# Moving 215 stores of a hybrid encoder layer from the sync queue to GpSimd's queue

## The chip, the cores and the metric

The kernel runs on one core of a Trainium2 chip. The metric is the device time of one execution in microseconds. A core has engines that run side by side, each through its own instruction list in order: TensorE (PE in the profile, PEld for its weight loads), VectorE (DVE), ScalarE (ACT), GpSimd (POOL) and SyncE (SP), which does nothing but issue transfers. A transfer between the chip's memory and the core's on-chip memory (a DMA) is started by an instruction in the list of SP, ACT or POOL; the issue takes a fraction of a microsecond there, and the bytes are moved by 16 DMA engines that all lists share. An instruction waits on semaphores until what it needs is there, and everything behind it in the same list waits with it.

## The reference

One layer of an encoder over 2048 positions of width 1024, in float32:

```python
u = _rms_norm(h, norm_mix_g[l])
proj = u @ w_in[l]
hy = _short_conv_centred(proj[..., :HY_COLS], hy_conv_w[l], hy_conv_b[l])
spec = _hyena_filter_spectrum(L, ...)          # filters from a small sine network, their rfft
y_hy = _group_rms_norm(_hyena(hy, spec, hy_skip[l]), hy_norm_g[l], HYENA_GROUPS)
qk = jax.nn.silu(_short_conv_centred(proj[..., HY_COLS:off], ml_conv_w[l], ml_conv_b[l]))
y_ml = _mlstm_bidirectional(q, k, v, o_pre, gates, ml_gate_b[l])
mixed = jnp.concatenate([y_hy, y_ml normed by group], axis=-1)
h = h + mixed @ w_out[l]
h = h + _cross_attention(_rms_norm(h, norm_x_g[l]), _rms_norm(mem, norm_mem_g[l]), ...)
h = h + jnp.square(jax.nn.relu(_rms_norm(h, norm_ff_g[l]) @ ff_w1[l])) @ ff_w2[l]
return _rms_norm(h, final_norm_g)
```

`_hyena` multiplies spectra twice (order 0 and 1): z is transformed, multiplied by the filter's spectrum, transformed back and gated. `_mlstm_bidirectional` is a linear recurrence over chunks with a matrix state per head, run forwards and backwards and summed.

## The kernel before

The large products run in float32 split into a rounded high part and a low part, three passes of TensorE each (`mm3`: L355, L358, L359); ScalarE makes the high parts and VectorE the low ones (L366).

Ahead of attention, two streams are woven together. The first is the input projection in halves of 1024 positions: `sweep` takes 256 columns at a time, keeps them channel-major, adds the width-3 convolution (L796 to L803), and `sweep_out` turns the result with TensorE (L825, L831, L845, L855) into staging tiles `st`, which go to memory: `hy` (convolved channels, L828 and L834), `qt` and `kt` (queries and keys, L837) and `kn` (keys the other way round, L849 and L858). `natural` projects values, output gates (`vd`, `od`, L896) and scan gates (`gt`, L903). The second stream is the filters (`filters`: their spectra leave as `fs` through `by_phase`, L339) and then `hyena`. In `hyena`, `spectrum` transforms eight blocks of z on TensorE, copies the result (L998) and stores it as `zs` (L339, through `by_phase`). When all blocks are there, a pass over 16 frequency blocks loads `zs` and `fs` (L920), transforms (L1030), multiplies by the filter (L1034 on VectorE, L1035 on GpSimd, their sum L1036 on VectorE), transforms back (L987), copies (L988) and stores `zg` (L989). Then `zg` is loaded again (L339 as a load), with the gate rows from `hy` (L974). This happens twice; the second time ends with the normed result `yh` (L1060 and L1066 on GpSimd, store L1068).

The gate scans (`gates`) give coefficient rows (`rows`, L1161 and L1162). `backward` makes the states of the backward recurrence from the last chunk to the first: GpSimd scales values (L1196), TensorE multiplies (L1200), VectorE adds (L1206), and the state goes out as `cbd` (L1219). `memproj` projects the memory for attention, with its weights loaded in `raw_stream` (L415). `mlstm` makes the outputs of 16 chunks; GpSimd multiplies rows (L1290), adds masks (L1291) and applies the output gate (L1343); after every second chunk the results are normed (VectorE, L1356) and stored as `ym` (L1358). Attention loads `yh` and `ym` (L1473); most of `mlstm` is woven with attention.

The program is written with a tile framework: a tile name has a fixed number of buffers, an instruction that writes into a used buffer waits until its readers (stores too) are done, and the framework adds those waits. A scheduler in that framework sets the order of each engine's list from a timeline of its own, so the order in the lists is not that of the code. Loads are issued by the sync queue. Before the change GpSimd issues the stores of `zg`, `vd`, `od`, of half the `zs`, and of the memory's projections (`gd`, `vw`); the sync queue issues the other stores of these stages.

Of the kernel before, what the change touches and what calls it, by code (L numbers as in the profile page):

```python
# [128 lines left out]
class Prog:  # L129
# [102 lines left out]
    def filters(self):  # L232
        nc, tc, a = self.nc, self.tc, self.a
        sd = [self.dram(f"fs{o}", (16, 64, 4, CH)) for o in range(2)]
        sb, ta, tb = self.fsb, self.ta, self.tb
        if True:
# [68 lines left out]
            def front(es, st, o, j2):  # L305
                pp = [self.hy() for q in range(4)]
                self.beside(*((pp[q][64 * jj + 32 * p:64 * jj + 32 * p + 32], f1[32 * q:32 * q + 32, 32 * p:32 * p + 32],
                               es[jj][p][32 * q:32 * q + 32]) for q in range(4) for jj in range(2) for p in range(2)))
                for h in range(2):
                    for i in range(2):  # L310
                        nc.scalar.copy(st[h][:, i], pp[2 * h + i])
                    self.by_phase(nc.sync, sd[o], j2, h, st[h])

            nxt = windows(0)
            for j2 in range(8):
# [499 lines left out]
    def sweep_out(self, ct, cv, t0, n):  # L815
# [3 lines left out]
        if ct < 12:  # L819
            w = min(n // 8, 128)  # L820
            dst = self.d_hy[ct // 4, t0:t0 + 8 * w, cc].rearrange("(q j) c -> q j c", j=8)
            for j4 in range(2):
                pt = self.mm().rearrange("p (k t) -> p k t", k=4)
                for jj in range(4):
                    nc.tensor.transpose(pt[0:w, jj], cv[:, 4 * j4 + jj:8 * w:8], self.ident)  # L825
                st = self.ist.tile([128, 4, 128], F32, tag="st", name="st", bufs=3)
                self.copy(st[0:w], pt[0:w])
                nc.sync.dma_start(out=dst[:, 4 * j4:4 * j4 + 4], in_=st[0:w])  # L828
            if n > 8 * w:
                pt = self.mm()  # L830
                nc.tensor.transpose(pt[0:16, 0:128], v[:, 8 * w:n], self.ident)  # L831
                st = self.ist.tile([128, 4, 128], F32, tag="st", name="st", bufs=3)
                self.copy(st[0:16, 0], pt[0:16, 0:128])
                nc.sync.dma_start(out=self.d_hy[ct // 4, t0 + 8 * w:t0 + n, cc], in_=st[0:16, 0])  # L834
            return
        h = ct % 4
        nc.sync.dma_start(out=(self.d_qt if ct < 16 else self.d_kt)[h, :, t0:t0 + n], in_=v)  # L837
        if ct < 16:
            return
        for b in range(0, n, 512):  # L840
            pt = self.mm().rearrange("p (k t) -> p k t", k=4)
            st = self.ist.tile([128, 4, 128], F32, tag="st", name="st", bufs=3)
            full = min(4, (n - b) // 128)
            for jj in range(full):
                nc.tensor.transpose(pt[:, jj], v[:, b + 128 * jj:b + 128 * jj + 128], self.ident)  # L845
            if full:
                self.copy(st[:, 0:full], pt[:, 0:full])
                r0 = t0 + b
                nc.sync.dma_start(out=self.d_kn[r0:r0 + 128 * full, cc].rearrange("(j q) c -> q j c", q=128),  # L849
                                  in_=st[:, 0:full])  # L850
            rest = min(512, n - b) - 128 * full
            if rest:
                s0 = b + 128 * full
                pt = self.mm()
                nc.tensor.transpose(pt[0:rest, 0:128], v[:, s0:s0 + rest], self.ident)  # L855
                st = self.ist.tile([128, 4, 128], F32, tag="st", name="st", bufs=3)
                self.copy(st[0:rest, 0], pt[0:rest, 0:128])
                nc.sync.dma_start(out=self.d_kn[t0 + s0:t0 + s0 + rest, cc], in_=st[0:rest, 0])  # L858

    def natural(self, hf, tiles, after=None, at=4):  # L860
        nc, a, sb = self.nc, self.a, self.isb
# [2 lines left out]
        for c2 in tiles:  # L864
# [3 lines left out]
            for t in range(8):  # L868
# [28 lines left out]
                if c2 == 3:  # L897
# [2 lines left out]
                    nc.vector.tensor_tensor(sg[:, t], p[:, 256:272], self.gb, ALU.add)  # L900
                    if t == 7:
                        dst = self.d_gt[1024 * hf:1024 * hf + 1024]
                        nc.sync.dma_start(out=dst.rearrange("(t p) g -> p t g", p=128), in_=sg)  # L903

    def hyena(self, es):
        nc, tc, a = self.nc, self.tc, self.a
# [84 lines left out]
        def spectrum(o, j2, z):  # L991
# [5 lines left out]
                for h in range(2):  # L997
                    (nc.vector.tensor_copy if h else nc.scalar.copy)(st[h][:, i], pp[2 * h + i])  # L998
            for h in range(2):
                self.by_phase(nc.sync if h else nc.gpsimd, sds[o], j2, h, st[h])  # L1000

        q, fq = [load1(0), load1(1)], []
        yield 52
# [9 lines left out]
        for o in range(2):  # L1013
# [27 lines left out]
            for j2 in range(8):  # L1041
# [34 lines left out]
    def gates(self):  # L1076
# [4 lines left out]
        with tc.tile_pool(name="m_g", bufs=1) as sg:  # L1081
# [79 lines left out]
            nc.sync.dma_start(out=rows[0], in_=negM)  # L1161
# [47 lines left out]
    def backward(self, sb, first, last, old, pin=None, lean=False):  # L1209
# [3 lines left out]
        for n in range(first, last, -1):  # L1213
# [13 lines left out]
    def mlstm(self, es):  # L1227
# [71 lines left out]
        for n in range(16):  # L1299
# [51 lines left out]
            if n % 2:  # L1351
                rv = self.bank_rsqrt(sb, ss, 128)
                for i, y in enumerate(ys):
                    t0 = 128 * (n - 1 + i)
                    for h in range(4):
                        nc.vector.scalar_tensor_tensor(y[:, h], y[:, h], rv[:, 4 * i + h:4 * i + h + 1],  # L1356
                                                       gml[:, 128 * h:128 * h + 128], ALU.mult, ALU.mult)
                    stores.append(lambda t0=t0, y=y: nc.sync.dma_start(  # L1358
                        out=ym[t0:t0 + 128].rearrange("t (h e) -> t h e", h=4), in_=y))
            if n < 14:  # L1360
                ld.append(loads(n + 2))
# [831 lines left out]
```

## Time and profile before

| | us |
|---|---|
| median of 3 runs | 3070.66 |
| lowest and highest run | 3070.19, 3076.88 |
| the profiled execution | 3074.8 |
| its span, from first to last instruction | 3073.1 |

| engine | busy us | share of the span |
|---|---|---|
| TensorE | 2981.7 | 97% |
| TensorE weight loads | 2367.8 | 77% |
| VectorE | 1947.8 | 63% |
| ScalarE | 1491.4 | 49% |
| GpSimd | 1213.7 | 39% |

In the profile a line such as `L339` is a line of the kernel; `a<-zg` says that tile a is written from tensor zg; `SPq` and `POOLq` are the lists of SP and POOL while they only wait or issue. Issuing does not count as busy. The granted clock is TensorE's, as a share of full speed. Attention begins at about 1170 us, and until about 1525 us the last chunks of `mlstm` are woven into it.

### The profile page before, as it was taken

To read this page: it belongs to the slowest core of one execution; us is meant where nothing else is said; L and a number is where in the kernel's file an instruction comes from. 1 tells how busy PE (TensorE), PEld (TensorE's weight loads), DVE (VectorE), ACT (ScalarE), POOL (GpSimd) and SP (SyncE) were. 2 spreads that over 40 slices of the span, in tenths; PEclk is the share of its full clock that TensorE was granted. 3 is DMA by queue.
4 is the path that set the end of the run, shared out by engine and by line. 5 is a ranking of instruction groups with operands and counts; after the bars stand their busy time and mean duration, and the time that the engine had idled before them with its cause. 6 is when DMAs were issued, how large, how long until landed. Compare 5 with 4: busy or idle time off the path is not lost.

```text
span 3073.1 us, 44126 instructions
## 1 busy us (share of the span) xinstructions
PE 2981.7 (97%) x14799; PEld 2367.8 (77%) x14799; DVE 1947.8 (63%) x3442; ACT 1491.4 (49%) x2930; POOL 1213.7 (39%) x942
## 2 busy tenths in 40 slices
PE   9999999998999898999999999999999999999998
PEld 7666667775678667888887888888888888888876
DVE  8855555556755547868665666558555676566695
ACT  6443455634754235555544455556555443333335
POOL 0112113310333544333133247765565374344653
PEclk9999999999999998999999999999999999999999
DMA  6655677586877986564567466657544565344434
GB/s 225 194 188 173 209 250 232 185 275 198 268 218 220 328 286 206 159 223 134 186 205 256 152 209 217 206 182 249 189 154 153 186 199 172 116 159 120 155 103 164
DMA packets 427867, 607.03 MB, mean 198 GB/s; under 512 B 38894, under 2 KB 232302, under 8 KB 426616
## 3 DMA queue, kind: packets, MB, share of 16 engines
q1 hardware_dynamic: 406644, 546.43, 55.6%
q0 software_dynamic: 12544, 41.95, 3.8%
q10 hardware_dynamic: 8452, 15.83, 1.4%
q8 instruction: 117, 1.92, 0.3%
q14 instruction: 110, 0.90, 0.1%
HBM read 401.67 MB, written 202.41 MB: 197 GB/s over the span
## 4 chain that ended last, share of the span: by engine, by line
PE 82%; DMA 7%; DVE 5%; issue 2%; ACT 2%; POOL 1%; SPq 1%; DVEq 0%; ACTq 0%; POOLq 0%
PE mm L355 17%; PE mm L358 17%; PE mm L359 17%; PE hy L359 6%; PE hy L355 6%; PE hy L358 6%; PE hy L173 2%; PE hy L1030 2%; PE mm L956 2%; PE hy L987 1%; DMA va<-vd 1%; DMA a<-zg 1%; PE hy L1322 1%; PE hy L1324 1%; PE mm L825 1%
## 5 line engine op out<-in xcount | busy, mean ns | idle before, releaser
L1692 ACT CAST ah<-w 128x512 fp32r<-128x512 f32 x284 | 176.5, 622 | 300.5 <-PE hy L358 155.9
L1693 DVE TENSOR_TENSOR bl<-wr,bh 128x512 fp32r<-128x512 f32 x213 | 240.0, 1131 | 125.4 <-ACT bh L1692 125.0
L366 DVE TENSOR_TENSOR wl<-wn,wh 128x512 fp32r<-128x512 f32 (+1 forms) x296 | 215.6, 772 | 90.9 <-ACT wh L366 90.6
L355 PE MATMUL mm<-xh,wh 128*128 128x512 f32 x640 | 266.6, 418 | 1.9 <-ACT xh L366 1.0
L358 PE MATMUL mm<-xl,wh 128*128 128x512 f32 x640 | 255.1, 399 | 4.6 <-DVE xl L366 4.6
L359 PE MATMUL mm<-xh,wl 128*128 128x512 f32 x640 | 254.4, 398 | 0.0
L1692 ACT CAST bh<-wr 128x512 fp32r<-128x512 f32 x232 | 143.6, 621 | 228.3 <-PE mm L359 174.3
L1693 DVE TENSOR_TENSOR al<-w,ah 128x512 fp32r<-128x512 f32 x236 | 217.4, 922 | 57.0 <-ACT ah L1692 57.0
L355 PE MATMUL mm<-bh,ah 128*128 128x512 f32 x576 | 225.8, 392 | 1.4 <-DVE acc L1854 1.3
L359 PE MATMUL mm<-bh,al 128*128 128x512 f32 x576 | 223.8, 391 | 3.4 <-DVE al L1693 3.4
L358 PE MATMUL mm<-bl,ah 128*128 128x512 f32 x576 | 224.9, 390 | 0.0
L366 ACT CAST wh<-wn 128x512 fp32r<-128x512 f32 (+1 forms) x296 | 164.6, 620 | 103.9 <-PE mm L359 50.1
L358 PE MATMUL mm<-act,wh 128*128 128x512 f32 x512 | 201.9, 394 | 0.0
L355 PE MATMUL mm<-act,wh 128*128 128x512 f32 x512 | 198.6, 394 | 1.4 <-ACT wh L366 1.3
L359 PE MATMUL mm<-act,wl 128*128 128x512 f32 x512 | 199.5, 392 | 0.1
L355 PE MATMUL hy<-bh,ah 128*128 128x512 f32 x448 | 175.2, 391 | 0.0
L358 PE MATMUL hy<-bl,ah 128*128 128x512 f32 x448 | 174.6, 390 | 0.0
L359 PE MATMUL hy<-bh,al 128*128 128x512 f32 x448 | 174.4, 390 | 0.0
L331 POOL TENSOR_TENSOR b<-b 128x512 f32<-128x512 f32 x32 | 48.1, 1504 | 293.3 <-DVE b L330 273.7
L355 PEld LDWEIGHTS mm<-xh,wh 128*128 128x128 f32 x640 | 121.6, 190 | 52.0 <-issue 21.2
L358 PEld LDWEIGHTS mm<-xl,wh 128*128 128x128 f32 x640 | 121.7, 190 | 51.3 <-issue 20.2
L355 PE MATMUL mm<-wh,xh 128*128 128x256 f32 (+1 forms) x512 | 155.1, 303 | 1.2 <-DVE a L960 1.2
(390 smaller groups left out, 8210.0 us busy)
## 6 DMA issues: line engine op xcount, KB each, us to landing
wr<-hc SPq DMA_DIRECT2D x224, 256.0 KB
w<-in_ff_w_dram SPq DMA_DIRECT2D x172, 256.0 KB
hc<-wn SPq DMA_DIRECT2D x128, 256.0 KB
wn<-in_w_in_dram SPq DMA_DIRECT2D x100, 256.0 KB
hc<-q SPq DMA_DIRECT2D x96, 256.0 KB
fs<-a SPq DMA_DIRECT2D x32, 512.0 KB
a<-fs SPq DMA_DIRECT2D x64, 256.0 KB
a<-zs SPq DMA_DIRECT2D x64, 256.0 KB
```

The source lines that it names most:

```text
L173: b = self.nc.tensor.matmul(*products[-1], start=True, stop=True)
L331: nc.gpsimd.tensor_tensor(b, f, b, ALU.subtract)
L355: first = mm(ps, lh, rh, start=start, stop=False)
L358: mm(ps, lh, rl, start=False, stop=False)
L359: self.last = mm(ps, ll, rh, start=False, stop=stop)
L366: both = (self.nc.scalar.copy(hi, src), self.nc.vector.tensor_tensor(lo, src, hi.bitcast(F32), ALU.subtract))
L825: nc.tensor.transpose(pt[0:w, jj], cv[:, 4 * j4 + jj:8 * w:8], self.ident)
L956: nc.tensor.matmul(pp, dm[:, m], t[:, m], start=True, stop=True)
L987: nc.tensor.matmul(pg, em[:, m], y, start=True, stop=True)
L1030: nc.tensor.matmul(pp, dm[:, m], t[:, m], start=True, stop=True)
L1692: self.nc.scalar.copy(hi, src)
L1693: eng.tensor_tensor(lo, src, hi.bitcast(F32), ALU.subtract)
```

## The change

Every store of the stages ahead of attention that the sync queue issued is now issued by GpSimd: `fs`, `hy`, `qt`, `kt`, `kn`, `gt`, the other half of `zs`, `yh`, `rows`, `cbd` and `ym`. The sync queue keeps the loads there, and the stores of attention and after it.

```diff
 filters
-                    self.by_phase(nc.sync, sd[o], j2, h, st[h])
+                    self.by_phase(nc.gpsimd, sd[o], j2, h, st[h])
 sweep_out
-                nc.sync.dma_start(out=dst[:, 4 * j4:4 * j4 + 4], in_=st[0:w])
+                nc.gpsimd.dma_start(out=dst[:, 4 * j4:4 * j4 + 4], in_=st[0:w])
-        nc.sync.dma_start(out=(self.d_qt if ct < 16 else self.d_kt)[h, :, t0:t0 + n], in_=v)
+        nc.gpsimd.dma_start(out=(self.d_qt if ct < 16 else self.d_kt)[h, :, t0:t0 + n], in_=v)
-                nc.sync.dma_start(out=self.d_kn[r0:r0 + 128 * full, cc].rearrange("(j q) c -> q j c", q=128),
+                nc.gpsimd.dma_start(out=self.d_kn[r0:r0 + 128 * full, cc].rearrange("(j q) c -> q j c", q=128),
...
 hyena, spectrum
-                self.by_phase(nc.sync if h else nc.gpsimd, sds[o], j2, h, st[h])
+                self.by_phase(nc.gpsimd, sds[o], j2, h, st[h])
 hyena, results
-                    nc.sync.dma_start(out=yh[q, :, js], in_=sq[phase[q]])
+                    nc.gpsimd.dma_start(out=yh[q, :, js], in_=sq[phase[q]])
 gates
-            nc.sync.dma_start(out=rows[0], in_=negM)
-            nc.sync.dma_start(out=rows[1], in_=inter)
+            nc.gpsimd.dma_start(out=rows[0], in_=negM)
+            nc.gpsimd.dma_start(out=rows[1], in_=inter)
 backward
-            self.nc.sync.dma_start(out=cbd[n - 1], in_=new.rearrange("d h e -> d (h e)"))
+            self.nc.gpsimd.dma_start(out=cbd[n - 1], in_=new.rearrange("d h e -> d (h e)"))
 mlstm
-                    stores.append(lambda t0=t0, y=y: nc.sync.dma_start(
+                    stores.append(lambda t0=t0, y=y: nc.gpsimd.dma_start(
```

The scheduler makes the lists anew. GpSimd's list gets 215 instructions more and the sync queue's 215 fewer; TensorE's, VectorE's and ScalarE's instructions are the same in number and differ in order in places up to about 1320 us. Three places follow.

GpSimd's list where the first pointwise pass of `hyena` begins. Before:

```order
L339 DMA zs_2736<-a 128x1024 x8
L1035 TENSOR_TENSOR b<-b,a 128x512 x3
L989 DMA zg_2738<-a 16x8x512 x2
L1035 TENSOR_TENSOR b<-b,a 128x512
L989 DMA zg_2738<-a 16x8x512
L1035 TENSOR_TENSOR b<-b,a 128x512
L989 DMA zg_2738<-a 16x8x512
```

and after:

```order
L837 DMA kt<-cv 128x1008
L849 DMA kn<-st 128x4x128
L849 DMA kn<-st 128x3x128
L1035 TENSOR_TENSOR b<-b,a 128x512 x2
L858 DMA kn<-st 112x128
L849 DMA kn<-st 128x4x128
L849 DMA kn<-st 128x3x128
L858 DMA kn<-st 112x128
L1035 TENSOR_TENSOR b<-b,a 128x512
L989 DMA zg_2738<-a 16x8x512 x2
L1035 TENSOR_TENSOR b<-b,a 128x512
```

The stores of keys, which wait for copies of the turned tiles, now stand between the products.

The sync queue's list where the second transform's blocks are handed over (zs_2737 is the second order's transform, fs_391 its filter). Before:

```order
L339 DMA zs_2737<-a 128x1024
L828 DMA hy<-st 128x4x128
L1161 DMA rows<-negM 128x128
L828 DMA hy<-st 128x4x128
L1162 DMA rows<-inter 128x128
L834 DMA hy<-st 16x128
L920 DMA a<-zs_2737 128x1x512 x2
L920 DMA a<-fs_391 128x1x512 x2
```

and after:

```order
L920 DMA a<-zs_2737 128x1x512 x2
L944 DMA dm<-in_c_dm_dram 128x256
L920 DMA a<-fs_391 128x1x512 x2
L920 DMA a<-zs_2737 128x1x512 x2
L949 DMA em<-in_c_em_dram 128x256
```

The stores that stood ahead of the first zs loads are gone from this list.

GpSimd's list in `mlstm`, around the end of the second chunk. Before:

```order
L1343 TENSOR_TENSOR ht<-ht,og 128x512
L739 DMA vw<-o 128x2x256 x3
L1291 TENSOR_TENSOR rw<-rw,mask_9881 128x512
L1290 TENSOR_TENSOR rw<-rw,qn 128x512
L1291 TENSOR_TENSOR rw<-rw,mask_9886 128x512
L1290 TENSOR_TENSOR rw<-rw,qn 128x512
L1343 TENSOR_TENSOR ht<-ht,og 128x512
```

and after:

```order
L1343 TENSOR_TENSOR ht<-ht,og 128x512
L1358 DMA ym<-ht 128x512 x2
L1291 TENSOR_TENSOR rw<-rw,mask_9881 128x512
L1290 TENSOR_TENSOR rw<-rw,qn 128x512
L1291 TENSOR_TENSOR rw<-rw,mask_9886 128x512
L1290 TENSOR_TENSOR rw<-rw,qn 128x512
L1343 TENSOR_TENSOR ht<-ht,og 128x512
```

The two stores of results, which wait for VectorE's norming (L1356), now stand ahead of the next chunk's mask additions; the last stores of the memory's values have moved to an earlier place.

More of the change, by code (lines that the diff above doesn't have):

```diff
@@ L833, in sweep_out @@
                 self.copy(st[0:16, 0], pt[0:16, 0:128])
-                nc.sync.dma_start(out=self.d_hy[ct // 4, t0 + 8 * w:t0 + n, cc], in_=st[0:16, 0])
+                nc.gpsimd.dma_start(out=self.d_hy[ct // 4, t0 + 8 * w:t0 + n, cc], in_=st[0:16, 0])
             return
         h = ct % 4
-        nc.sync.dma_start(out=(self.d_qt if ct < 16 else self.d_kt)[h, :, t0:t0 + n], in_=v)
+        nc.gpsimd.dma_start(out=(self.d_qt if ct < 16 else self.d_kt)[h, :, t0:t0 + n], in_=v)
         if ct < 16:
@@ L857, in sweep_out @@
                 self.copy(st[0:rest, 0], pt[0:rest, 0:128])
-                nc.sync.dma_start(out=self.d_kn[t0 + s0:t0 + s0 + rest, cc], in_=st[0:rest, 0])
+                nc.gpsimd.dma_start(out=self.d_kn[t0 + s0:t0 + s0 + rest, cc], in_=st[0:rest, 0])
     def natural(self, hf, tiles, after=None, at=4):
@@ L902, in natural @@
                         dst = self.d_gt[1024 * hf:1024 * hf + 1024]
-                        nc.sync.dma_start(out=dst.rearrange("(t p) g -> p t g", p=128), in_=sg)
+                        nc.gpsimd.dma_start(out=dst.rearrange("(t p) g -> p t g", p=128), in_=sg)
     def hyena(self, es):
```

## The prediction

> **What bounds the kernel now.** I read the page first, then the windows by stage, then who waits for whom, on TensorE and on the sync queue.
>
> ```profile
> span 3073.1 us, 44126 instructions
> PE 2981.7 (97%) x14799; PEld 2367.8 (77%) x14799; DVE 1947.8 (63%) x3442; ACT 1491.4 (49%) x2930; POOL 1213.7 (39%) x942
> PE 82%; DMA 7%; DVE 5%; issue 2%; ACT 2%; POOL 1%; SPq 1%; DVEq 0%; ACTq 0%; POOLq 0%
> ```
>
> TensorE is the bound: 97% of the span, and 82% of the chain that ended last. What a change of queues can win or lose is TensorE's idle time in the stages whose stores move. The windows (columns: the stretch in us; its length; the busy times of TensorE, its weight loads, VectorE, ScalarE and GpSimd, with their instructions; granted clock; DMA share; GB/s) show where that is:
>
> ```profile
> 0.00:100.00 100.00, 97.46 (x432) 78.53 (x433) 83.90 (x208) 68.85 (x128) 0.68 (x6) 0.98 0.69 227
> 100.00:350.00 250.00, 243.68 (x1504) 164.35 (x1502) 154.27 (x239) 104.74 (x175) 48.14 (x32) 0.99 0.51 169
> 350.00:700.00 350.00, 336.84 (x1948) 248.87 (x1949) 192.63 (x305) 183.98 (x322) 83.68 (x96) 0.99 0.77 246
> 700.00:750.00 50.00, 37.33 (x205) 22.92 (x204) 39.39 (x145) 23.61 (x41) 2.14 (x4) 0.91 0.67 211
> 750.00:1000.00 250.00, 246.63 (x1261) 183.45 (x1260) 152.13 (x259) 142.09 (x240) 87.50 (x90) 0.99 0.74 226
> 1000.00:1150.00 150.00, 138.03 (x695) 103.40 (x694) 66.98 (x206) 47.24 (x132) 78.80 (x78) 0.98 0.93 306
> 1150.00:1200.00 50.00, 36.32 (x215) 32.66 (x216) 35.98 (x124) 26.50 (x100) 18.91 (x16) 0.83 0.68 226
> ```
>
> Length less the first number, summed over the seven rows, is 2.5 + 6.3 + 13.2 + 12.7 + 3.4 + 12.0 + 13.7 = 63.8 us: the ceiling of any gain. The fourth row is the gate stage, where a serial chain on VectorE rules (39.4 of 50 us). In the sixth the DMA engines are 93% busy. The sync queue does wait in front of its stores, with loads behind them (columns: total us, times, longest):
>
> ```profile
> SPq L339 <- ACT a L311: 77.2, 25, 11.5
> SPq L828 <- ACT st L201: 55.2, 21, 5.8
> SPq L1358 <- DVE ht L1356: 24.9, 14, 6.1
> SPq L837 <- ACT cv L801: 23.0, 3, 11.2
> ...
> PE hy L1030 <- DMA a<-zs: 8.8, 3, 4.4
> ...
> PE hy L987 <- DVE b L1036: 2.1, 1, 2.1
> ```
>
> The four sync rows make 180 us of waiting, but the costliest wait of TensorE for a load is 8.8 us, and that one is for a store to land and its data to be read back. The loads behind the held stores are mostly early enough. So I expect little from freeing the sync queue, and look for what the GpSimd queue costs.
>
> **The change part by part.** By the code it moves 215 stores: 32 of the filters, 60 of the convolution (48 full, 12 of 16 rows), 16 of queries and keys, 24 of transposed keys, 2 of gates, 16 of the forward transforms, 32 and 16 of the two results, 2 of rows, 15 of states. No bytes change.
>
> ```profile
> L828 SPq DMA_DIRECT2D hy<-st x48: 309/371/1860, 73.3 to 743.3; - x48
> L989 POOL DMA_DIRECT2D zg<-a x64: 530/553/631, 437.2 to 953.7; - x64
> L896 POOL DMA_DIRECT2D od<-st x16: 717/740/764, 473.1 to 1006.7; - x16
> ```
>
> Issuing (ns, least/median/most): 371 on sync, whatever the pieces; on GpSimd 553 for 128 pieces of a row and 740 for 256, so 0.19 us per further 128 pieces. A store of 512 pieces (hy, kn) is not in the trace as a GpSimd store; below it is no cheaper than the 740 ns row, above four times 553 = 2.2 us; I take 0.74 + 2 x 0.19 = 1.1 us, on the line of the two rows. All 215 then take some 150 us of GpSimd's time, against 880 us in which it is not busy before 1200 us (the seven rows show it busy 320 us). The issue time as such is covered; what counts is what stands behind it.
>
> *First hand-over of the transforms, 411 to 420 us.* The last zs stores must land before the first zs load:
>
> ```profile
> 413.99 0.34 SPq L339 DMA_DIRECT2D zs<-a  x1
> ...
> 416.83 1.17 SPq L920 DMA_DIRECT2D a<-zs  x2
> ...
> DMA to landing us min/median/max: 3.4/3.5/3.5
> ```
>
> From the sync queue the last store was landed after at most 416.83 - 413.99 = 2.84 us; the two GpSimd zs stores of these same microseconds took 3.4 to 3.5 (third row, zs on line 339 between 400 and 425 us). TensorE waits at this point, so the change costs **+0.6**; at most +1.5 with the longer issue ahead of it.
>
> *Second hand-over, 740 us.* Here the sync queue itself is late:
>
> ```profile
> 740.28 0.33 SPq L339 DMA_DIRECT2D zs<-a  x1
> ...
> 742.00 1.18 SPq L1161 DMA_DIRECT2D rows<-negM  x1
> ...
> 745.24 1.17 SPq L920 DMA_DIRECT2D a<-zs  x2
> ...
> 740.41 0.54 POOL L339 DMA_DIRECT2D zs<-a  x1 [6.05 <-ACT a L998]
> ```
>
> The last landing is that of the GpSimd store. It took 3.9 us:
>
> ```profile
> DMA to landing us min/median/max: 3.9/3.9/3.9
> ```
>
> So the data was there at 744.3, and the load went out at 745.24, behind five hy and rows stores. After the change both zs stores go out one behind the other on GpSimd (740.3 and 740.8), the second lands at 744.7, and no store holds the load: **-0.5** (between -0.9 and 0).
>
> *Products behind stores.* In the two pointwise passes GpSimd multiplies (L1035) for VectorE's sum (L1036), which feeds TensorE's L987. Between the products the changed order puts 14 full kn stores (1.1 us each), 8 partial (0.5), 7 of queries and keys and 6 of states (0.55 each, as 128 pieces) and one of the gates (1,024 pieces, 1.9): 15.4 + 4 + 3.9 + 3.3 + 1.9 = 28 us, in what was 64 products and their zg, od and vd stores.
>
> ```profile
> L1035 POOL TENSOR_TENSOR b<-b,a x64: 1262/1293/3907, 423.6 to 944.9; 128x512 f32<-128x512 f32 x64
> ...
>   ACT b L1033: 90.7, 43
> ...
>   DVE b L1036: 14.2, 32
> ```
>
> GpSimd was idle 90.7 us ahead of 43 of its 64 products, 2.1 us each, waiting for ScalarE: about half of the stores fall into that. The other 14 us come late to VectorE, which waited for half of the products already (32 of 64, 14.2 us in all). Of those 14.2 us TensorE felt 2.1 (row L987 above), 15%. At the same share 14 us cost **+2**; the bounds are 0 (all hidden) and +14 (VectorE passes on all of it).
>
> By the Trainium skill (SBUF — State Buffer, "SBUF: two separate sides") a VectorE operation in a two-port mode locks GpSimd out of the port with which it writes descriptors, so that its DMAs wait. The trace has 64 zg stores in stages where VectorE is busy 55 to 60%, and none took over 631 ns to issue, so it does not bear the rule out; if the rule held, the result would be that of rival D.
>
> *Results of the recurrence.* Two ym stores now stand in GpSimd's queue behind L1343 of each second chunk, ahead of the masks (L1291) of the next, and wait for VectorE's eight L1356:
>
> ```profile
> 1153.74 1.26 POOL L1291 TENSOR_TENSOR rw<-rw,mask 128x512 f32<-128x512 f32 x1 [3.58 <-DVE hy L215]
> ...
> 1160.88 1.27 POOL L1291 TENSOR_TENSOR rw<-rw,mask 128x512 f32<-128x512 f32 x1 [4.66 <-DVE rw L1275]
> ...
> 1155.36 2.89 DVE L1356 SCALAR_TENSOR_TENSOR ht<-ht,hy,gml 128x128 f32<-128x128 f32 x8
> ...
> 1164.16 0.69 DVE L1294 TENSOR_TENSOR rw<-rw,hy 128x512 f32<-128x512 f32 x1 [0.47 <-PE hy L1284]
> ...
> 1157.20 1.40 SPq L1358 DMA_DIRECT2D ym<-ht x2
> ...
> 1159.26 1.14 ACT L1336 ACTIVATE ht<-hy,den 128x128 f32<-128x128 f32 x4 [2.95 <-DMA ym<-ht]
> ```
>
> The first mask add moves from 1153.74 to 1158.25 + 2 x 0.55 = 1159.3, 5.6 us later; its exponential takes 1.3 and is wanted at 1164.16, so it hides. The second moves from 1160.88 to 1161.8. ScalarE's L1336 waits for the first ym landing, 2.06 us after issue on sync; with 3.4 it starts about 1 us later. Later chunks stand between attention's products. I take **+0.5** (0 to +8, a microsecond for each of 8 pairs).
>
> *Loads ahead of attention, 1000 to 1150 us.* From the sync queue go 32 yh stores of 128 KB and 15 cbd stores of 258 KB, with their loads behind:
>
> ```profile
> cbd<-cb SPq DMA_DIRECT2D x15, 258.0 KB
> ...
> yh<-a SPq DMA_DIRECT2D x32, 128.0 KB
> ```
>
> These 8 MB still cross the same DMA engines, which are 93% busy, so mostly they compete from another queue. TensorE idles 12.0 us here; the gain lies between 0 and -12, and I take **-1**, near zero, because of that DMA share.
>
> The filter stores (32 fs, 48 hy) I cost at nothing: TensorE idles 6.3 us in 250 there, and the GpSimd subtraction (L331) is idle-rich (48 of 250 us busy). If that cover goes, a front product waits one store and copy, 1 to 2 us, at up to 16 places.
>
> Sum: 0.6 - 0.5 + 2 + 0.5 - 1 = +1.6. The profiled execution took 3074.8 (span 3073.1), 4.1 over the median of 3070.66; it would become 3076.4, and the median **3072**. A measurement here tells 0.2%, 6.1 us, from no change.
>
> **The rivals.** *A: GpSimd's queue becomes the bound (slower).* The 14 us of late products reach TensorE, since VectorE works in order and its next casts of weights wait as well; ym adds 1 us in some pairs. For it: VectorE waits for half of the products already. Against: only 15% of that reached TensorE. It shows as slower once VectorE passes on about 45% (6 of 14). Full price +14 + 0.6 - 0.5 + 1 = +15: 3086. Chance 0.22.
>
> *B: the sync queue was the brake (faster).* Loads of projection weights, keys and values reach their tiles earlier in 1000 to 1150 us; of the 12.0 us idle there 8 to 10 go, and of the 13.2 in 350 to 700 some 2. For it: the 180 us of held sync queue. Against: the DMA share. 3070.66 - 10 = 3061. Chance 0.20.
>
> *C: the order, not the queue.* The scheduler also orders TensorE's filter and projection products anew before 1140 us. The idle time of those rows (6.3 and 12.0) may move by a half each way: plus or minus 9, 3062 or 3080. Chance 0.10, half to each side.
>
> *D: VectorE starves GpSimd's stores (slower).* One L1035 of the row above took 3907 ns, 2.6 over its median. If each of the 36 stores between products were stretched so, 94 us more would stand ahead of products; at 15% +14: 3085. Against: 631 ns at most in 64 stores. Chance 0.04. This is what the page on SBUF cited above would make of it.
>
> That the stores do not move is excluded: GpSimd gains 215 instructions, the sync queue loses 215.
>
> **How the numbers follow.** My forecast, no change that can be told, 0.44, with its own range of 3065 to 3077 (3070.66 less half of the 12.0, with nothing against it, and plus half of the 14 less a half, with nothing for it). A and D and half of C make slower 0.31; B and half of C faster 0.25. The range reaches to B's price below and A's above: 3060 to 3087.
>
> **What would show it.** Right: the zg and new hy and kn issues at 0.5 to 1.2 us; the first zs load 0.5 to 1 us later after the last zs store; TensorE's idle time before 1200 us within 6 us of 63.8; waits for L1035 on VectorE (14.2) up by some 10. Wrong by A or D: that wait over 30 us, or stores above 2 us each. Wrong by B: the row of 1000 to 1150 us with 145 or more busy. Wrong by C: idle time moved in 100 to 350 us, with no GpSimd or sync wait ending it.

## The result, and the profile after

The changed kernel is slower. Its median is 3092.79 us (3085.71 to 3094.59) against 3072.51 (3070.19 to 3076.88) of the kernel before, run in turn with it: a ratio of 1.0055, with a 95% interval of 1.0043 to 1.0068, some 17 us. The forecast was 3072, no change, with a range of 3060 to 3087. The time lies above the range.

The page of the profiled execution of the changed kernel (3092.18 us), its first rows:

```profile
span 3090.5 us, 44177 instructions
PE 2990.0 (97%) x14799; PEld 2375.7 (77%) x14799; DVE 1949.0 (63%) x3442; ACT 1493.9 (48%) x2930; POOL 1349.1 (44%) x1157
```

The span grew by 17.4 us. TensorE's instructions are the same 14,799, and yet their busy time grew by 8.3 us (2981.7 to 2990.0); only the other 9.1 us are idle time. The same work took longer as the granted clock was lower, which the views of cores show (span, mean granted TensorE clock), first of the kernel before, then of the changed one:

```profile
core 0: 3073.1 us, clock 0.988
```

```profile
core 0: 3090.5 us, clock 0.983
```

In the trace's record the granted clock is 1.0 or 0.5, so the mean gives the time at half: 2 x 0.012 x 3073.1 = 74 us before and 2 x 0.017 x 3090.5 = 105 us after, each give or take 3 for the rounding. The windows by stage of the changed kernel, to be laid beside those of the prediction:

```profile
0.00:100.00 100.00, 95.99 (x431) 76.78 (x432) 83.45 (x207) 68.96 (x128) 8.67 (x16) 0.98 0.67 225
100.00:350.00 250.00, 244.44 (x1502) 166.17 (x1501) 154.67 (x240) 103.35 (x172) 93.00 (x101) 0.98 0.49 168
350.00:700.00 350.00, 332.82 (x1917) 245.26 (x1916) 191.51 (x302) 184.79 (x322) 108.58 (x135) 0.98 0.76 245
700.00:750.00 50.00, 40.46 (x238) 25.39 (x238) 37.39 (x141) 21.56 (x37) 11.53 (x19) 0.93 0.58 206
750.00:1000.00 250.00, 239.41 (x1162) 174.84 (x1163) 155.15 (x255) 143.17 (x239) 102.07 (x117) 0.97 0.71 220
1000.00:1150.00 150.00, 144.94 (x748) 111.19 (x747) 62.36 (x190) 38.41 (x90) 94.85 (x114) 0.98 0.91 309
1150.00:1200.00 50.00, 28.37 (x158) 25.93 (x157) 33.66 (x115) 29.44 (x114) 20.65 (x18) 0.73 0.54 177
```

TensorE's idle time before 1200 us is 73.6 us, against 63.8. The rows cannot be compared one by one, since the program is 13 us late by 1000 us and stages slide over the borders. Cut after equal numbers of TensorE's matmuls instead, the profiles differ from the one before as follows (us; the borders are those of the kernel before; the other columns are experiments below, e13 the changed kernel again). One execution of e5 took 6062.61 us, in a slower state, and is in no median, ratio or profile here.

| stage | after | e13 | e1 | e2 | e10 | e6 |
|---|---|---|---|---|---|---|
| 0 to 362 | 1.5 | 0.9 | 1.5 | 3.6 | 5.3 | 0.5 |
| 362 to 477 | 4.2 | 2.9 | 3.5 | -1.9 | -1.6 | -0.6 |
| 477 to 798 | -0.4 | 0.8 | -0.3 | -0.8 | 2.8 | -1.6 |
| 798 to 856 | 6.9 | 4.8 | 0.8 | 3.3 | 3.9 | 1.2 |
| 856 to 1146 | 0.9 | -1.8 | 3.9 | -4.4 | -6.1 | -1.9 |
| 1146 to 1200 | 4.7 | 5.8 | 1.4 | 6.1 | 0.2 | 3.3 |
| behind 1200 | -0.3 | 2.4 | -0.6 | -0.8 | -0.7 | -3.5 |
| all | 17.4 | 15.8 | 10.2 | 5.0 | 3.8 | -2.7 |

Each column is one execution, and these executions lie up to 5 us from the median of their kernel (e1's is 4.8 above, e2's 4.9 below; among all runs one of e3 lies 10.6 above), so only what comes back in several columns says anything. The loss of the changed kernel lies in three short places: 362 to 477, 798 to 856, and 1146 to 1200 us. The first of them is not firm: e5 and e12, which share the changed kernel's queues and lists up to there, have -1.9 and 0.2 in it.

In the third TensorE multiplies the same products in the same order in both kernels, so its windows can be compared, first of the kernel before, then of the changed one:

```profile
1146.39:1200.04 53.65, 39.76 (x247) 35.91 (x245) 37.14 (x128) 29.11 (x111) 21.84 (x19) 0.84 0.69 223
1159.45:1217.78 58.33, 42.38 (x246) 37.88 (x246) 41.55 (x140) 32.08 (x121) 25.01 (x22) 0.81 0.55 182
```

Of the 4.7 us, 2.1 are idle time and 2.6 go with the lower granted clock; in e13 0.9 and 4.9, at a clock of 0.74.

What the sync queue waits for in the changed kernel (total us, times, longest):

```profile
SPq L395 <- DVE wl L366: 186.9, 45, 26.4
...
SPq L949 <- PE hy L987: 147.9, 23, 13.9
...
SPq L292 <- DMA fs<-a: 73.4, 9, 15.6
```

The stores that held it are gone, and it now waits longer at its loads (the first two rows were 63.7 and 113.7 us before), for the buffers that these fill. From TensorE's waits before 1200 us in the changed kernel:

```profile
PE hy L1030 <- DMA a<-zs: 11.2, 3, 5.7
PE hy L1322 <- DVE den L1330: 5.8, 1, 5.8
...
PE mm L845 <- DVE a L960: 2.1, 2, 1.8
PE mm L855 <- ACT st L891: 1.7, 1, 1.7
```

None of these four ends with an instruction of GpSimd, though the first waits for data that GpSimd's stores have to bring out. The fourth is in no row of the kernel before. L1322 stopped there too, but for other results of VectorE:

```profile
PE hy L1322 <- DVE ht L1356: 4.3, 1, 4.3
...
PE hy L1322 <- DVE bry L213: 3.1, 1, 3.1
```

### The profile page after: what moved, and what is told of

It reads as the page before. It is cut to its first block, busy times and chain, and to the rows that moved or that the text cites. A ratio compares the mean times of both kernels' runs of the same rounds, so it can differ in the third digit from the quotient of the medians.

```text
span 3090.5 us, 44177 instructions
## 1 busy us (share of the span) xinstructions
PE 2990.0 (97%) x14799; PEld 2375.7 (77%) x14799; DVE 1949.0 (63%) x3442; ACT 1493.9 (48%) x2930; POOL 1349.1 (44%) x1157
## 4 chain that ended last, share of the span: by engine, by line
PE 56%; DVE 2%; DMA 2%; ACT 1%; issue 1%; POOL 0%; SPq 0%; DVEq 0%; POOLq 0%; ACTq 0%
PE mm L355 12%; PE mm L359 12%; PE mm L358 12%; PE hy L359 6%; PE hy L355 6%; PE hy L358 6%; PE hy L1322 1%; PE hy L1324 1%; PE hy L1284 0%; DVE bl L1693 0%; PE hy L1596 0%; PE hy L1479 0%; DVE acc L1991 0%; PE hy L1200 0%; DMA wr<-xs 0%
## 5 line engine op out<-in xcount | busy, mean ns | idle before, releaser
L359 PE MATMUL mm<-xh,wl 128*128 128x512 f32 x640 | 255.8, 400 | 0.0
L359 PE MATMUL mm<-bh,al 128*128 128x512 f32 x576 | 223.7, 391 | 4.0 <-DVE al L1693 4.0
L359 PE MATMUL mm<-act,wl 128*128 128x512 f32 x512 | 199.4, 391 | 0.0
L359 PE MATMUL hy<-bh,al 128*128 128x512 f32 x448 | 174.4, 390 | 0.0
L359 PE MATMUL mm<-wh,xl 128*128 128x256 f32 (+1 forms) x512 | 151.8, 297 | 0.0
```

What stands on the lines that cost most here:

```text
L359: self.last = mm(ps, ll, rh, start=False, stop=stop)
```

## The experiments

The change does two things at once: other queue for 215 stores, and new lists for all engines, which the scheduler made from it. To part them, some kernels hold the lists: edges of issue order alone, with no wait, chain each engine's instructions in the order of a table. "Old lists" are those of the kernel before (TensorE, VectorE, ScalarE, and the order among the instructions that do not move on GpSimd and sync), "new lists" those of the changed kernel. Every run was compared with the kernel before on the same chip; all of them compute the full result. The traces of e1 and e2 show the instructions of TensorE, VectorE and ScalarE in exactly the order of the kernel whose lists they hold. No run holds the old lists with nothing else changed; e6, which comes nearest, is 0.10% longer, so holding by itself costs hardly more than that.

| run | stores moved | lists | ratio (95% interval) | median us |
|---|---|---|---|---|
| e1 | all 215 to GpSimd | old | 1.0029 (1.0018 to 1.0040) | 3080.24 |
| e2 | none | new | 1.0037 (1.0025 to 1.0050) | 3084.71 |
| e3 | 152 of fs, hy, qt, kt, kn, gt, zs, rows | scheduler's | 1.0025 (1.0014 to 1.0036) | 3077.87 |
| e4 | 63 of yh, cbd, ym | scheduler's | 1.0020 (1.0011 to 1.0030) | 3078.63 |
| e7 | 47 of yh, cbd | old | 1.0014 (1.0005 to 1.0023) | 3074.78 |
| e9 | the other 168 | old | 1.0026 (1.0017 to 1.0035) | 3078.14 |
| e8 | yh, cbd to ScalarE | old | 1.0050 (1.0038 to 1.0062) | 3085.02 |
| e11 | 32 of gd, vw, from GpSimd to sync | old | 1.0015 (1.0006 to 1.0024) | 3075.85 |
| e10 | none | new to 998 us, then old | 1.0035 (1.0022 to 1.0048) | 3080.07 |
| e6 | none | new from 998 to 1150 us, with one piece mended, else old | 1.0010 (1.0002 to 1.0018) | 3072.58 |
| e5 | all | new, one piece mended | 1.0046 (1.0033 to 1.0060) | 3081.61 |
| e12 | all | new, two pieces mended | 1.0044 (1.0032 to 1.0057) | 3087.43 |
| e13 | all | new (the changed kernel again) | 1.0051 (1.0038 to 1.0065) | 3088.48 |

### Queue and lists apart: e1 and e2

```diff
 e1: the whole change, and
+    hold_order(tc)      # table: the lists of the kernel before
 e2: no store moved, and
+    hold_order(tc)      # table: the lists of the changed kernel
```

> All 215 stores are issued by GpSimd, as in the changed kernel, but the lists of TensorE, VectorE and ScalarE, and the relative order of everything else on GpSimd and the sync queue, are held to the order of the kernel before. Theory Q (the queue: what GpSimd issues goes out and lands later, and what stands behind it waits): the loss of the changed kernel stays, +12 to +20 us against before. Theory O (the order: the scheduler's new lists put TensorE's instructions where their operands are not ready): the loss goes, within 6 us of before. A mixture of both would lie between, at +6 to +12.

> No store is moved, but the lists of TensorE, VectorE and ScalarE, and the relative order of everything else on GpSimd and the sync queue, are held to the order of the changed kernel. Theory Q: within 6 us of before. Theory O: the whole loss, +12 to +20 us, with the same places of TensorE idle as the changed kernel (some 9 us behind the stop at 834 us, some 12 between 1090 and 1217 us).

Both halves cost by themselves, 0.29% and 0.37%; together 0.66%, against the 0.55% of the change, which the intervals allow. One place shows both at work, the first hand-over of the transforms, where TensorE's L1030 waits for the first zs load. In the order before, changed, e1, e2, from the timelines:

```profile
420.27 2.06 PE L1030 MATMUL hy<-a,dm 128*128 128x512 f32 x2 [3.33 <-DMA a<-zs]
```

```profile
426.72 2.05 PE L1030 MATMUL hy<-a,dm 128*128 128x512 f32 x2 [5.71 <-DMA a<-zs]
```

```profile
425.17 2.08 PE L1030 MATMUL hy<-a,dm 128*128 128x512 f32 x2 [4.07 <-DMA a<-zs]
```

```profile
423.19 2.05 PE L1030 MATMUL hy<-a,dm 128*128 128x512 f32 x2 [5.11 <-DMA a<-zs]
```

The queue alone adds 0.74 us (3.33 to 4.07; e9 has 3.89), the lists alone 1.78 (e10 1.51). In the other runs with unmoved stores and old lists at this place (e4, e6, e7, e8, e11) the wait is 3.26 to 3.55, and in the other runs with moved stores and new lists (e3, e5, e12, e13) 5.55 to 5.81.

### Early and late stores: e3 and e4

```diff
 e3: nc.sync -> nc.gpsimd for fs, hy, qt, kt, kn, gt, zs, rows alone
 e4: nc.sync -> nc.gpsimd for yh, cbd, ym alone
```

> Only the stores ahead of 1000 us are moved (fs, hy, qt, kt, kn, gt, zs, rows: 152 in all), with the scheduler free. In the trace of the changed kernel TensorE is 12.8 us behind the kernel before at its instruction 5250 (988 us before). Theory Q: +8 to +13 us. Theory O: the lists are made anew once more, so anything between -5 and +13, and the stop at 834 us need not show.

> Only the stores behind 955 us are moved (yh, cbd, ym: 63), with the scheduler free. In the changed kernel TensorE wins 7.6 us against before between its instructions 5250 and 5750 and loses 12.5 between 5750 and 6250. Theory Q: both again, +3 to +7 us. Theory O: the gain of 7 us without the loss is possible, so anything between -8 and +7.

No single group carries the loss: each half costs 0.20 to 0.25%, with lists that the scheduler made for it.

### The queue's half: e9, e7, e8 and e11

```diff
 e9: old lists; all but yh and cbd moved
 e7: old lists; L1068 and L1219 alone:
-                    nc.sync.dma_start(out=yh[q, :, js], in_=sq[phase[q]])
+                    nc.gpsimd.dma_start(out=yh[q, :, js], in_=sq[phase[q]])
-            self.nc.sync.dma_start(out=cbd[n - 1], ...)
+            self.nc.gpsimd.dma_start(out=cbd[n - 1], ...)
 e8: the same two with nc.scalar
 e11: old lists; gd and vw (L727, L739): nc.gpsimd -> nc.sync
```

> Lists held to the kernel before; of the stores only yh and cbd (47, in the stage where the DMA engines are 91 to 93% busy) are issued by GpSimd. Theory Q1 (a store on a queue of its own no longer stands behind the loads; where the DMA engines are full it takes their time at once, and the loads of values that TensorE waits for land later): the two stops of TensorE at L1200 grow from 2.7 and 1.8 us to about 6.6 and 3.3, as with all stores moved and the old lists, and one stop of 4 us at L725 goes: +2 to +5 us. If the loss of the moved stores comes from the earlier stages: within 2 us of before.

> Lists held to the kernel before; all moved stores but yh and cbd (168) are issued by GpSimd: what the run with yh and cbd alone leaves out. If the prices of the queue add up (all 215: +0.29%, yh and cbd alone: +0.14%): +0.15%, some +3 to +6 us, with the larger stops ahead of 430 us (at L173 for the blocks of hy, at L1030 for zs). If the 215 stores cost only together: within 2 us of before.

> The same two groups, yh and cbd, on ScalarE's queue in place of GpSimd's, lists held to the kernel before. Theory Q1 (any second queue does it): as in the run before this, +2 to +5 us, with the stops at L1200 of the same size. Theory Q2 (it is GpSimd's queue: its stores go out behind GpSimd's own work and hold up the scalings L1196): -3 to +1 us, with the stops at L1200 near 2.7 and 1.8 us.

> The opposite change in the stage where the DMA engines are full: lists held to the kernel before, no store moved to GpSimd, and the 32 stores of the memory's projections (gd, vw), which GpSimd issues in the kernel before, issued by the sync queue. Theory Q1 (a second queue with stores makes the loads land later): the va loads between 1030 and 1090 us come to use sooner than the 6.6 to 9.4 us of before, the two stops at L1200 shrink, and the time is -1 to -4 us. Against it: these stores then hold loads back on the sync queue while they wait for ScalarE's copies: +2 to +6 us.

The prices of the two parts, 0.26% and 0.14%, make 0.40%, where e1 has 0.29% for both at once; the intervals allow either, so no more than the order of size is known of each.

The measure here is how long a load of values (va, 256 KB, sync queue, L1184) takes to reach the GpSimd product that waits for it (L1196), in the stretch where the DMA engines are over 90% busy. The second of three such loads, from the timelines of SyncE and GpSimd, in e11, before and e1:

```profile
1050.58 1.45 SPq L1184 DMA_DIRECT2D va<-vd  x1
...
1058.58 1.05 POOL L1196 TENSOR_TENSOR va<-va,cols 128x516 f32<-128x516 f32 x1 [12.55 <-DMA va<-vd]
```

```profile
1051.08 1.68 SPq L1184 DMA_DIRECT2D va<-vd  x1
...
1060.46 1.03 POOL L1196 TENSOR_TENSOR va<-va,cols 128x516 f32<-128x516 f32 x1 [9.83 <-DMA va<-vd]
```

```profile
1055.09 1.21 SPq L1184 DMA_DIRECT2D va<-vd  x1
...
1067.30 1.04 POOL L1196 TENSOR_TENSOR va<-va,cols 128x516 f32<-128x516 f32 x1 [7.96 <-DMA va<-vd]
```

| GpSimd's stores in this stretch | kernels | us from issue to product, the three loads, mean over the kernels |
|---|---|---|
| none | e11 | 7.0 |
| gd, vw | before, e2, e3, e6, e9, e10 | 7.9 |
| gd, vw, yh, cbd | after, e1, e4, e5, e7, e12, e13 | 10.3 |

The bytes are the same in all of them. So the loads land later the more stores go out from a second queue. That a store on the loads' own queue stands behind them, and from a second queue takes its share of the DMA engines at once, fits this; the traces show the landing and not whose turn it was. TensorE then waits at the states' products, in the kernel before and in e1:

```profile
1072.24 1.23 PE L1200 MATMUL hy<-va,kn 128*128 128x129 f32 x4 [2.70 <-DVE a L1064]
...
1089.79 1.16 PE L1200 MATMUL hy<-va,kn 128*128 128x129 f32 x8 [1.78 <-POOL va L1196]
```

```profile
1079.14 1.23 PE L1200 MATMUL hy<-va,kn 128*128 128x129 f32 x4 [6.61 <-DVE a L1064]
...
1098.79 1.16 PE L1200 MATMUL hy<-va,kn 128*128 128x129 f32 x8 [3.33 <-POOL va L1196]
```

The second stop is a wait for L1196 itself. The first goes by a longer way: L1060 stands behind L1196 in GpSimd's list, VectorE's L1062 and L1064 wait for L1060, and the stop ends 11.8 us behind the start of L1196 in both kernels. With yh and cbd alone moved (e7) the two are 4.36 and 1.96. In the changed kernel the loads take as long as in e1's group (10.3 us), but its lists put other work in this place, and L1200 stops there for 0.2 us only (1.1 in e13). So these stops are the price of the queue under the old lists; where late loads cost in the changed kernel itself is not shown. Its stage from 856 to 1146 us, with 0.9 and -1.8, is 3 to 5 us behind e2's -4.4, which has the same lists and no moved store. At 360 to 385 us, where stores of filters and transforms go out, the changed kernel's GpSimd queue carries 5.0 MB instead of 2.1, with the DMA engines full in both; but TensorE's stop there (L173, 1.49 us before) lies anywhere between 0.35 (e5) and 2.99 (after) among kernels with the same queues and lists, so nothing is read from it.

ScalarE's queue is worse, though a different place pays. In e8's timeline four yh stores take 8.18 us to issue while the sync queue issues loads into the same full engines, and ScalarE's copies (L715) stand behind them. The issue is half of the 16.4 us for which ScalarE stood idle ahead of L715:

```profile
1067.45 8.18 ACTq L1068 DMA_DIRECT2D yh<-a  x4
1068.22 9.54 SPq L974 DMA_DIRECT2D a<-hy  x4
...
1076.39 5.78 PE L708 MATMUL mm<-mt,wm 128*128 128x256 f32 x13 [10.78 <-ACT o L715]
```

e11 was to gain 1 to 4 us, by the theory that loads alone decide. The loads did land sooner, and L1200's stop of 2.70 shrank to 0.60, but the time rose by 0.15%. That theory is too short. What ScalarE's copies L715 waited for, in e11 and in the kernel before, and TensorE's longest stop in e11's stretch:

```profile
  DMA gd<-o: 60.1, 12
```

```profile
  DMA gd<-o: 20.8, 8
```

```profile
1082.44 3.78 PE L725 MATMUL mm<-kt,wm 128*128 128x256 f32 x8 [5.64 <-ACT o L715]
```

L715 writes into tiles that the gd stores must first have read. On the sync queue these stores now land later, ScalarE waits 60.1 us for them instead of 20.8, and TensorE waits for these copies, which it did not in the kernel before. The sync queue also waits 16.2 us in front of its new stores (L739), with loads behind them; how much each of the two costs was not tried. Measured is that moving yh and cbd to GpSimd (e7) and moving gd and vw to the sync queue (e11) both cost some 0.15%; the kernel before, between the two, is the fastest of the three.

### The lists' half: e10 and e6

```diff
 e10: no store moved; table: new lists up to 998 us, old behind
 e6: no store moved; table: old lists up to 998 us, new to 1150 us (with e5's mend), old behind
```

> No store is moved. The lists are those of the changed kernel up to 998 us and those of the kernel before from there on. The whole new order without moved stores cost +0.37%, some 11 us. Theory O2 (the order costs ahead of 998 us, above all by the stops at L845 and L855 near 830 us and the half clock behind them): +3 to +7 us. Theory O3 (it is all behind 998 us): within 2 us of before.

> No store is moved. The lists are those of the kernel before up to 998 us and from 1150 us on, and between them those of the changed kernel, with the four L1194 set back as in the run before this. Theory O1: of the order held without moved stores (+11 us), the part ahead of 998 us (+3 in its profile) and the stop at 1138 us are gone, and what stays is its gain between 1011 and 1090 us: -4 to -8 us against before. If the loss between 1090 and 1165 us hangs on the whole piece of the lists and not on L1194: 0 to +5 us.

The early lists carry nearly all of the half, 0.35%. The late ones gained 1.9 us up to 1146 us in e6's profile and gave back 3.3 in the stage behind, at a granted clock of 0.78 against 0.84; the time is 0.10% longer.

What the early lists do can be seen near 830 us. The timeline of e2, where no store has moved:

```profile
827.75 0.63 PE L845 MATMUL mm<-ident,cv 128*128 128x128 f32 x4 [1.80 <-DVE a L960]
...
830.96 1.12 PE L1030 MATMUL hy<-a,dm 128*128 128x512 f32 x2 [1.58 <-DMA a<-zs]
...
839.34 0.28 PE L855 MATMUL mm<-ident,cv 128*16 128x128 f32 x1 [1.67 <-ACT st L891]
```

In the kernel before, the first two stops are 1.07 and 1.10 us and the third does not exist. In the new list of ScalarE the copies L891 stand behind L988, L1032 and L1033; in the old one they stood ahead of L988. All kernels with these lists (after, e2, e3, e5, e10, e12, e13; in e12 this piece is mended, see below) have the first stop at 1.80 to 1.82 and the third at 1.67 to 2.16, whatever the queues; none with the old lists has the third. The second stop belongs to neither list: it lies between 0.48 and 1.58 with the new ones and between 0.87 and 2.39 with the old.

### Single pieces mended: e5, e12 and e13

```diff
 e5, ScalarE's list near 1150 us
-L1194 ACTIVATE ve<-va,cols x4
 L1327 ACTIVATE hy<-hy x2
 L1349 ACTIVATE junk<-ht x4
+L1194 ACTIVATE ve<-va,cols x4
 e12: e5's edit, and ScalarE's list near 845 us
+L891 COPY st<-mm x2
 L988 COPY a<-hy
 L1032 ACTIVATE b<-hy
 L1033 COPY b<-hy
-L891 COPY st<-mm x2
 e13: the changed kernel, unedited
```

> The changed kernel with its own lists on all engines held as they are, but for one piece of ScalarE's: the four scalings L1194 of one early chunk of the recurrence, which stand ahead of the next L1327 and wait 5.8 us there for their values to be loaded, are set back behind four L1349, as in the kernel before. Theory O1 (this piece makes the stop of TensorE at 1151 us, 5.8 us, and its slow clock after it): 4 to 8 us less than the changed kernel, so +9 to +13 us against before, and the wait of L1194 for va falls from 19.8 to under 14 us. If something else makes that stop (the load itself, or L1200, which needs L1194's result): within 2 us of the changed kernel, +15 to +18.

> The changed kernel with its own lists held but for two pieces of ScalarE's: the four L1194 set back (as in the run with that piece alone), and near 845 us two copies L891 put ahead of L988, L1032 and L1033, as in the kernel before, so that the bank that TensorE's L855 needs comes free while TensorE still multiplies. Theory O1 (such pieces are what the new order costs): the stop of 1.67 us at L855 goes, with the half clock that follows it, and the time is 2 to 5 us below the run with one piece: +9 to +12 us against before, 5 to 8 below the changed kernel. If the stop only moves to another place: within 2 us of the run with one piece (+12 to +16).

> The changed kernel once more, beside the run with two pieces mended: +14 to +21 us against before as in its first timing, and in its profile the same stops at L1030 (5.7 us near 420), L845 (1.8) and L855 (1.67) near 830 to 845, and at L1322 (5.8 near 1150). What differs between its two profiles at a place with the same lists is the error with which a single profile can be read: I expect 1 to 3 us for a stage.

In the changed list ScalarE's L1194 waits for a load of values, and everything behind it waits too. The timeline of e2 shows the pair:

```profile
1140.23 1.28 ACT L1194 ACTIVATE ve<-va,cols 128x129 f32<-128x129 f32 x4 [5.77 <-DMA va<-vd]
...
1143.67 0.77 PE L1322 MATMUL hy<-va,rw 128*128 128x129 f32 x2 [5.91 <-DVE den L1330]
```

In e5 L1194 waits for nothing, and the stop falls to 1.60 us, but the next piece stops instead:

```profile
1143.73 0.46 PE L1322 MATMUL hy<-va,rw 128*128 128x129 f32 x2 [1.60 <-DVE den L1330]
1147.22 2.09 PE L1200 MATMUL hy<-ve,kn 128*128 128x129 f32 x8 [2.37 <-ACT ht L1336]
```

The stop lies just ahead of the border at 1146 us of the table above. From 856 to 1200 us together e5 is 1.6 us behind the kernel before, against 5.6 and 4.0 in the two profiles of the changed kernel; but e12, with the same piece mended, is 4.9 behind. The whole kernel gained perhaps 2 to 3 us (1.0046 against 1.0055 and, in e13, 1.0051, with intervals that overlap): not the expected gain. e12 missed too, and its timeline tells why. Its L891 copies were put first, and still came late:

```profile
836.38 0.79 POOL L849 DMA_DIRECT2D kn<-st  x1
...
842.19 0.65 ACT L891 COPY st<-mm 128x256 f32<-128x256 f32 x2 [5.36 <-DMA kn<-st]
842.62 0.28 PE L855 MATMUL mm<-ident,cv 128*16 128x128 f32 x1 [1.70 <-ACT st L891]
```

L891 writes into a staging tile that the kn store must first have read, and that store lands 5.7 us after its issue. In the kernel before, L891 starts 4.9 us after the like store of the sync queue (828.85 to 833.76). The store itself also goes out later: 4.5 us behind the start of L845 (831.92 to 836.38), against 2.7 in the kernel before (826.12 to 828.85). So the list made L891 late in e2, and with the list mended the store on GpSimd's queue does, by its issue and its landing; whether the mended list with the stores on the sync queue would lose the stop was not tried. Against e13, in the same comparison, e12 is 1 us shorter, which cannot be told from nothing.

## Why the prediction was wrong, point by point

**The sum left the lists at nothing.** This is the step that failed first. The forecast costed each store by its queue, and put the scheduler's new order into rival C, at plus or minus 9 us and a chance of 0.10. By itself the order costs 0.37%, 11 us (e2; by its interval 8 to 15). So the 9 us were nearly the size, and the step that failed is that they stood beside the sum and not in it. Half of the idle time in two rows was also no ceiling, since an order can add stops where none had been (L855, 1.67 us). The sign that the text named for rival C, idle time moved between 100 and 350 us, did not show in the changed kernel (5.6 us against 6.3): the order cost elsewhere.

**Loads ahead of attention: -1, with the wrong sign.** The text saw that the 8 MB "still cross the same DMA engines" and concluded that little changes. What it missed is which bytes go first. The loads' way to GpSimd grew from 7.9 to 10.3 us, e7 costs 0.14%, and under the old lists L1200's two stops grew from 4.5 to 9.9 us (e1). Rival B (freeing the sync queue gains) falls: e1, e7 and e9 are all slower. The row that was to show it, 145 us or more busy from 1000 to 1150 us, came to 144.94, but only because the stages slid: over the same stage, 856 to 1146 us of the kernel before, TensorE idles 12.1 us, against 12.3.
The Trainium skill has the rule that the prediction should have weighed (DMA: Bandwidth & Descriptors, "Queues, rings and completion order"): each DMA engine goes round-robin over the queues that have work for it. The runs agree in what follows from it, with the 7.0, 7.9 and 10.3 us above.

**Idle time was taken as the whole price.** All bounds were counted in idle microseconds of TensorE. The change added 9.1 of them and 8.3 more that go with the lower clock. The timeline of the changed kernel at 832 us shows how:

```profile
832.10 0.63 PE L845 MATMUL mm<-ident,cv 128*128 128x128 f32 x4 [1.81 <-DVE a L960]
...
834.78 2.07 PE L1030 MATMUL hy<-a,dm 128*128 128x512 f32 x2 [1.05 <-DMA a<-zs]
...
839.22 0.41 PE L359 MATMUL mm<-wh,xl 128*128 128x256 f32 x1
...
840.48 0.28 PE L359 MATMUL mm<-wh,xl 128*128 128x256 f32 x1
```

After the two stops L1030 takes 2.07 us where it takes 1.12 in e2 above, and the products of L359 0.41 instead of 0.28, up to 840.4 us.

**First hand-over: +0.6.** Right in size for the queue (0.56 to 0.74 by e9 and e1), but in part by luck: the last store landed there after 2.9 us, not 3.4 to 3.5, and the load went out 3.2 us behind it, against 2.84 before. The lists' 1.78 were not in the sum.

**Second hand-over: -0.5.** Right as far as the queue goes: TensorE's wait there was 4.37 us before, 3.95 in e1 and 3.94 in e9. With the new lists it is 4.46 in the changed kernel and 4.14 in e13.

**Issue times.** Right in kind, high in size. Stores of 512 pieces were put at 1.1 us; the groups of the changed kernel (ns, least/median/most) give 0.8:

```profile
L828 POOL DMA_DIRECT2D hy<-st x48: 757/805/1042, 73.6 to 747.4; - x48
```

All 215 add 1349.1 - 1213.7 = 135 us to GpSimd (the profile counts an issue as busy time on GpSimd, unlike on the sync queue), forecast 150, and they found room. Rival D falls: no store that GpSimd issued in the changed kernel took over 1.04 us to issue, where 2 would have shown it. What the estimate did not ask is how long the new stores take to land and so to free their tiles (e12).

**Products behind stores: +2.** Too high; nothing of it shows. The line of L1035 in the changed kernel says what its engine waited for and who waited for it:

```profile
  ACT b L1033: 65.3, 38
...
  DVE b L1036: 15.0, 30
```

GpSimd's idle time ahead of its products shrank from 90.7 to 65.3 us, where the stores went, and VectorE's wait rose from 14.2 to 15.0 us, not by 10. TensorE's wait for L1036 fell from 2.1 to 1.3. Rival A (that wait over 30 us) falls, though its 3086 lies near the outcome: the price was near, the mechanism was not.

**Results of the recurrence: +0.5, filter stores: 0.** Not to be told from zero: behind 1200 us the differences are -0.3 (after), 2.4 (e13) and -0.6 (e1). In the first 362 us the changed kernel and e1 both lose 1.5; the prediction had 0 with up to 1 to 2 us a place.

**Left open.** Why the scheduler's new early lists cost as much as they do is shown at two places only (in e2 the first hand-over, +1.8, and near 830 us, 0.7 + 1.7 = +2.4), less than half of e2's 11. That the rest is many short stops of the same kind is argued, not shown; putting single pieces right (e5, e12) moved the time by 1 to 3 us, no more than the comparisons can tell. Nothing that was run beats the kernel before.

## What to carry to other kernels

When a scheduler sets the lists, the price of an edit is the edit's plus that of the new lists, and the second can be the larger; run the edit with held lists, and the new lists without the edit, before either is explained. Before a store is moved off a queue, ask what it stood behind there: on a queue of its own it competes with loads that it used to let pass, and where DMA is full the loads land later. Long waits of an issuing queue are no price; only TensorE's waits for the loads behind them are, and where the granted clock falls behind such stops, they can cost about twice their length (here 9.1 us of idle time came with 8.3 us of slower work).

## What the runs showed of the hardware that was not expected

*The clock.* Half clock came after stops of 1.81 and 1.05 us with 1.6 us of work between them (granted clock 0.54 from 834 to 841 us in the changed kernel's windows), while the same kernel in its other profile (e13), with stops of 1.80 and 1.05 us at the same instructions, kept 1.00 over 826 to 842 us. e2, with 1.80 and 1.58, kept it over 826 to 848 us, as did e12 with 1.82 and 0.66. So the same stops bring it or not. The Trainium skill (TensorE: Matmul & The Clock Gate, "Part 1: The HAM clock gate") says that the gate judges by free-running windows of some 3.4 us, so that its phase differs between executions; the trace agrees in that equal stops came out both ways. The rule drawn from it there, no idle gaps above some 3.4 us ("HAM oscillation — how this bites in real kernels"), is too wide for these two stops, which add up to 2.9 us.

*Issue from ScalarE.* Four yh stores took 8.18 us to issue from ScalarE's queue while the sync queue was issuing loads (9.54 us for four), where GpSimd issues one such store in 0.50 us (489 to 564 ns over 32 in e1). So with the DMA engines full (a share of 1.04 from 1067 to 1076 us of e8) the issue itself took longer on these two queues, and on ScalarE that holds its computing; on GpSimd none of this was seen.
